# Two pairs of the up projection in two by two steps, with the sums over x1 made in pieces and x1 kept in DRAM

## The chip, the core and the metric

One core of one Trainium2 chip. The metric is the device time of one execution in microseconds, as the median over runs.

## The reference

One layer of a gated convolution and attention block with a convolutional feed-forward part, on 512 positions of width 1024 in float32:

```python
h = rms_norm(x, norm_mix_g[l]);  proj = h @ w_in[l]
... # a gated short convolution and an attention, merged by two gates
x = x + (g_conv * y_conv + g_attn * y_attn) @ w_o[l]
h = rms_norm(x, norm_ffn_g[l])
up = causal_dwconv(h @ w_up[l], conv_ffn_w[l])      # w_up: 1024 x 5632
a, b = jnp.split(up, 2, axis=-1)
x = x + (jax.nn.silu(a) * b) @ w_down[l]            # w_down: 2816 x 1024
...
return rms_norm(x, norm_f_g)
```

## The kernel before

Features lie on the 128 partitions, positions along the free axis; x is 8 blocks of 128 x 512. Float32 products are made of three passes of matmuls: each operand is split into a high and a low part (`wh`, `wl` for weights, `x1h`, `x1l` for the input of the up stage), and high x high, low x high and high x low are added in PSUM. A matmul is 128 x 128 by 256 columns.

**The stream of weights.** All weight chunks stand in one list, `stream`, in the order of use (`in`, `mix`, `wo`, `up`, then `P` and `F` chunks, `dp`). `load` fetches the raw chunk (5 buffers, SP's queue); `split` makes the high part on ACT (`wh_...`) and the low part on DVE (`wl_...`), each with two buffers, so the high part of chunk n+2 is made when PE is through with chunk n. `later` is a list of small pieces of work that `split` lets go behind its own instructions when their turn has come.

**Two by two steps.** Where a stage uses them, two blocks of outputs and two halves of the positions are multiplied by seven products instead of eight (`PROD`, helper `pair`). They need sums of the inputs (four quarter tiles t1 to t4, then their high and low parts) and sums of the weights. The weight sums are made in DRAM, as copies on SP's queue and accumulating transfers on POOL's (`group`, list `todo`), one operation at a time at each `tick`. A step reads a `P` chunk (plain weights) and an `F` chunk (sums). The gates 2 to 7 (`gs`) and most of the down projection (`dn`) are done so; the seven products end in four banks, `p23`, `p45`, `p16`, `p7`, which DVE and ACT put together.

**The wo stage** adds the merged product to x, block by block (`p_wo`): DVE makes x1 (L960), ACT the high part (L961) and the square (L915), DVE the low part (L962), POOL adds the squares to `ssq2` (L916). x1 stays in SBUF.

**The up stage** has 22 pairs of blocks, 0 to 11 in the first phase, each with one block for a and one for b. `block` makes 48 matmuls; with `lead` it does the first two row blocks' eight matmuls with the high weights ahead of the four with `wl`. The first two blocks, up0 and up1, are made by the helper `lead`, which calls `mid` between its parts: there the four matmuls `pc_n2` sum `ssq2` over the partitions, ACT takes the root (a table load and `rb_n2`, L1160) and DVE the reciprocal (L1161). `up` multiplies each block by the norm (`fz`, L992) and applies the three taps (`fu`, L585 on ACT, L586 and L589 on DVE); `glu` takes the silu and POOL or DVE the product; sums of pairs of these (L1022 to L1032) feed the down steps. Each down step adds its banks to x1 (`combine`).

**The end.** The last two blocks of the down projection are made directly, in two halves of the positions (`plain7`). Their sums of squares give the last norm (`fin_sum`, `fin_col`), and `fin_out` multiplies and sends a half away. For the first half the last of four products is POOL's, which reads a copy `rs` of the norm.

**The start.** For the second weight chunk of v (k = 1) DVE casts the first 264 columns (L247) and ACT the other 256 (L249); the matmuls `pa` read the first, `pb` the other. Tile, the layer in which this is written, sets the order of each engine's instructions, except where `keep` holds it; each engine works its list in order.

Of the kernel before, what the change touches and what calls it, by code (L numbers as in the profile page):

```python
# [8 lines left out]
F32 = mybir.dt.float32  # L9
# [4 lines left out]
P = 128  # L14
# [48 lines left out]
def block_kernel(ctx, tc, xT, vecs, wv, win, wmix, wo, wup, wst, wdp, outT):  # L63
# [10 lines left out]
    def keep(ins):  # L74
        return tc.keep_in_program_order(ins)
# [43 lines left out]
    groups = [[NFF + 2 * j, NFF + 2 * j + 1] for j in range(KB - GS)]  # L119
    ngate = len(groups)  # L120
    groups += [list(range(n, min(n + 2, NFF - 1))) for n in range(0, NFF - 1, 2)] + [[NFF - 1]]
    nstep = [len(d) for d in STEPS[0] + STEPS[1]] + [2] * (2 * (KB - GS))
    todo = []
# [26 lines left out]
    for i0, i1 in ((0, ngate), (ngate, len(groups))):  # L150
        for i in range(i0, i1, 3):
            todo += [op for ops in zip(*(group(x) for x in range(i, min(i + 3, i1)))) for op in ops]

    def tick():
        if todo:
            todo.pop(0)()

    def double(n):
        h = nstep[n]
        return [(f"P{n}", wst[n, :, : 3 * h * P], 3 * h * P), (f"F{n}", sums[n][:, : 4 * h * P], 4 * h * P)]  # L160

    def gate_n(j):
# [13 lines left out]
    for ph, (j0, j1) in enumerate(PHASES):  # L176
        stream += [(f"up{j}", wup[j], D) for j in range(2 * j0, 2 * j1)]
        for _ in STEPS[ph]:
            stream += double(n)
            n += 1  # L180
# [48 lines left out]
    def split(hl=None):  # L229

        k = len(parts)
        if k == len(stream):
            return
        nm, _, ncol = stream[k]
        load(k + (LOOK if k >= gs0 else AHEAD))
        if k >= gs0 and (nm[0] in "imwu" or nm[0] == "F" and int(nm[1:]) % 2):
            tick()
        if hl is None:
            hl = []
            for x in "hl":  # L240
                if k == 0:
                    wp.tile([P, PADW[x]], F32, tag=f"pad{x}", name=f"pad_{x}")
                hl.append(wp.tile([P, D], F32R, tag=f"w{x}", name=f"w{x}_{nm}", bufs=2)[:, :ncol])
        hi, lo = hl
        raw = raws[k]
        if k < 2:
            keep(nc.vector.tensor_copy(hi[:, :VW], raw[:, :VW]))  # L247
            if k:
                keep(nc.scalar.activation(hi[:, VW:], raw[:, VW:], AF.Copy))  # L249
# [7 lines left out]
        ins = nc.vector.tensor_sub(lo, raw, hi.bitcast(F32))  # L257
# [5 lines left out]
        run_later(k, {"u": 1.7, "P": 1.6, "F": 0.75, "d": 0}.get(nm[0], 3.5))  # L263

# [111 lines left out]


    ab = ExitStack()
    abp = ab.enter_context(tc.tile_pool(name="abp", bufs=1))
    abp.tile([P, PADL], F32, tag="pad", name="pad_ab")  # L380
    xgh = abp.tile([P, KB, S], F32R, tag="xgh", name="xgh")
    xgl = abp.tile([P, KB, S], F32R, tag="xgl", name="xgl")
    oth = abp.tile([P, 4, S], F32R, tag="oth", name="oth")
# [82 lines left out]
    for kb in range(KB):  # L466
# [16 lines left out]
        for cs in cuts:  # L483
            keep(nc.vector.scalar_tensor_tensor(
                xgl[:, kb, cs], x_of(kb, cs), g1(kb), xgh.bitcast(F32)[:, kb, cs],
                op0=ALU.mult, op1=ALU.subtract,
            ))
# [324 lines left out]
    def mt(name):  # L812
        return mp.tile([P, S], F32, tag="mt", name=name, bufs=5)

# [87 lines left out]
    xp = ctx.enter_context(tc.tile_pool(name="xp", bufs=1, side="right"))  # L902
    x1 = xp.tile([P, KB, S], F32, tag="x1", name="x1")
    x1h = xp.tile([P, KB, S], F32R, tag="x1h", name="x1h")
# [47 lines left out]

    po = None
    for j in range(KB):
        if j == 0:
            po = lead(["wo0", "wo1"], mh, ml)
        p = po[j] if j < 2 else block(f"wo{j}", mh, ml)
        xr = mt(f"xr{j}")
        nc.gpsimd.dma_start(xr, xT[:, j, :])
        nc.vector.tensor_add(x1[:, j, :], p, xr)  # L960
        nc.scalar.activation(x1h[:, j, :], x1[:, j, :], AF.Copy, scale=col(G2 + j))  # L961
        nc.vector.scalar_tensor_tensor(  # L962
            x1l[:, j, :], x1[:, j, :], col(G2 + j), x1h.bitcast(F32)[:, j, :],
            op0=ALU.mult, op1=ALU.subtract,
        )
        square_into(ssq2, x1[:, j, :], j == 0, mp, f"sq2_{j}")
    mg.close()
# [3 lines left out]
    fp = ctx.enter_context(tc.tile_pool(name="fp", bufs=1))  # L971
    fp.tile([P, PADL], F32, tag="pad", name="pad_f")

# [6 lines left out]

    acc = ring(*range(6))
    ssq3 = xp.tile([P, S], F32, tag="ssq", name="ssq3")

    def place(ph, q):
        return (q - PHASES[ph][0] // 2) * (NF + ph)

    def up(j, rb2, pu=None):
        uu = []
        for s_ in range(2):
            p = pu[s_] if pu else block(f"up{2 * j + s_}", x1h, x1l, True)  # L990
            z = fp.tile([P, S], F32, tag="fz", name=f"fz{j}{s_}", bufs=2)
            nc.vector.tensor_mul(z, p, rb2)  # L992
# [57 lines left out]
    def combine(ph, i, banks, ids):  # L1050
# [5 lines left out]
        def z1():  # L1056
            t["z"] = fp.tile([P, S], F32, tag="fz", name=f"cz{ph}{i}", bufs=2)
            nc.scalar.activation(t["z"][:, th[0]], p16[:, th[0]], AF.Copy)
            nc.vector.tensor_add(t["z"][:, th[1]], p16[:, th[1]], t["z"][:, th[0]])
# [4 lines left out]
        def u3():  # L1064
            t["u"] = fp.tile([P, S], F32, tag="fz", name=f"cu{ph}{i}", bufs=2)[:, : 2 * P]
            nc.vector.tensor_add(t["u"], p7, t["z"][:, th[1]])
            nc.vector.tensor_add(m1[:, th[1]], p45[:, th[1]], m1[:, th[1]])
# [17 lines left out]
    def final_square(m):  # L1085
# [8 lines left out]
        nc.scalar.activation(y, y, AF.Copy, scale=col(GF + m))  # L1094

    final_square.first = True
    X, Y = (6, 7, 0, 1), (2, 3, 4, 5)
    open_ = {}

    def down(ph, n0):  # L1100
# [13 lines left out]
        for n, (name, prods) in enumerate(todo):  # L1114
# [98 lines left out]
    def fin_sum(t, m):  # L1213
# [8 lines left out]
        nc.scalar.activation(sq, r, AF.Square)  # L1222
        nc.scalar.activation(y, r, AF.Copy, scale=col(GF + m6 + m))
        return sq
# [7 lines left out]
    def fin_out(t, rc):  # L1232
        hs = halves[t]
        pb = rstd_bc(rc, 2, (1, 4)[t], f"n3{t}")[:, : S // 2]
        if t == 0:
            rs = fp.tile([P, S], F32, tag="fu", name="rs", bufs=3)[:, : S // 2]
            keep(nc.scalar.activation(rs, pb, AF.Copy))
        for g in range(4):
            y = x1[:, 2 * g : 2 * g + 2, hs]
            e, r = (nc.gpsimd, rs) if t == 0 and g == 3 else (nc.vector, pb)  # L1240
            keep(e.tensor_mul(y, y, r.unsqueeze(1).to_broadcast([P, 2, S // 2])))
        for g in range(4):
# [10 lines left out]
    for m in range(2):  # L1253
        plain7(m, 0, kall)
    sqA = [fin_sum(0, 0), fin_sum(0, 1)]
    plain7(0, 1, kall)
    plain7(1, 1, kall[:3])
    rcA = fin_col(0, sqA)
    sqB = [fin_sum(1, 0)]
    plain7(1, 1, kall[3:6])  # L1260
    fin_out(0, rcA)
    plain7(1, 1, kall[6:])
    sqB.append(fin_sum(1, 1))
# [10 lines left out]
def _layout(i):  # L1274
# [51 lines left out]
    for j in range(GS, KB):  # L1326
        for d in range(2):
# [42 lines left out]
```

## Time and profile before

| | |
|---|---|
| median of 3 runs | 697.62 us (697.56 to 697.66) |
| profiled execution | 697.7 us, span 695.9 us |
| PE busy | 686.7 us (99% of the span), 5976 matmuls |
| DVE, ACT, POOL busy | 508.5, 347.7, 158.4 us |
| wo stage | 295 to 338.4 us |
| up, first phase, from | 338.4 us |
| first phase of down | 470.9 to 528 us |
| granted TensorE clock | 0.999 |
| DMA | 118.91 MB, mean 171 GB/s |

Stages are read from the chain in order of time. A row of the timeline has start and duration in us, engine, line of the kernel, operation, output<-inputs by the program's names, shapes, a count (neighbours of one kind are merged) and, in brackets, the idle time before it with what ended it. PEld is the loading of weights, which overlaps PE. A row of a window has its length, the busy time of PE, PEld, DVE, ACT and POOL with counts, the granted clock, the busy share of the DMA engines and GB/s. A row of the groups has the count, the busy time and the mean in ns, then the idle time before.

### The profile page before, as it was taken

To read this page: it belongs to the slowest core of one execution; us is meant where nothing else is said; L and a number is where in the kernel's file an instruction comes from. 1 tells how busy PE (TensorE), PEld (TensorE's weight loads), DVE (VectorE), ACT (ScalarE), POOL (GpSimd) and SP (SyncE) were. 2 spreads that over 40 slices of the span, in tenths; PEclk is the share of its full clock that TensorE was granted. 3 is DMA by queue.
4 is the path that set the end of the run, shared out by engine and by line. 5 is a ranking of instruction groups with operands and counts; after the bars stand their busy time and mean duration, and the time that the engine had idled before them with its cause. 6 is when DMAs were issued, how large, how long until landed. Compare 5 with 4: busy or idle time off the path is not lost.

```text
span 695.9 us, 14568 instructions
## 1 busy us (share of the span) xinstructions
PE 686.7 (99%) x5976; PEld 684.8 (98%) x5976; DVE 508.5 (73%) x807; ACT 347.7 (50%) x553; POOL 158.4 (23%) x179
## 2 busy tenths in 40 slices
PE   8999999999999999999999999999999999999996
PEld 8999999999999999999999999999999999999996
DVE  6678777786687777755387777777684678777785
ACT  6674656554654444444444444445433354445663
POOL 5124646434011001025312212140000212020000
PEclk9999999999999999999999999999999999999999
DMA  8527877567359968768547647488677544433623
GB/s 309 190 86 203 208 154 179 136 172 176 96 147 255 261 178 231 245 187 211 149 110 195 186 120 213 114 177 229 199 210 223 145 99 129 123 96 104 191 78 122
DMA packets 54434, 118.91 MB, mean 171 GB/s; under 512 B 4928, under 2 KB 24384, under 8 KB 54368
## 3 DMA queue, kind: packets, MB, share of 16 engines
q1 hardware_dynamic: 39072, 96.55, 43.1%
q0 software_dynamic: 14576, 20.75, 18.7%
q8 instruction: 47, 0.77, 0.5%
q10 hardware_dynamic: 720, 0.69, 0.3%
q14 instruction: 19, 0.16, 0.1%
HBM read 115.80 MB, written 35.13 MB: 217 GB/s over the span
## 4 chain that ended last, share of the span: by engine, by line
PE 94%; DVE 2%; ACT 2%; issue 1%; DMA 1%; ACTq 0%; SPq 0%; DVEq 0%
PE p_up L286 26%; PE p_in L286 14%; PE dn L304 13%; PE gs L304 8%; PE p_up L304 8%; PE p_wo L286 6%; PE yc L304 3%; PE ya L286 3%; PE p_g L286 2%; PE o L675 2%; PE pa L494 2%; PE pb L496 1%; PE tp L660 1%; PE pdB L286 1%; PE pdA L286 1%
## 5 line engine op out<-in xcount | busy, mean ns | idle before, releaser
L286 PE MATMUL p_up<-x1l,wh_up 128*128 128x256 f32 x536 | 104.5, 276 | 0.0
L286 PE MATMUL p_up<-x1h,wh_up 128*128 128x256 f32 x536 | 104.4, 276 | 0.0
L286 PE MATMUL p_up<-x1h,wl_up 128*128 128x256 f32 x536 | 104.3, 276 | 0.0
L253 ACT ACTIVATE wh_up<-raw_up 128x1024 fp32r<-128x1024 f32 x44 | 46.7, 1060 | 81.8 <-PE p_up L286 68.7
L139 POOL DMA_DIRECT2D sum<-in_wst_dram x51 | 52.7, 1109 | 124.8 <-DMA sum<-sum 88.1
L286 PEld LDWEIGHTS p_up<-x1l,wh_up 128*128 128x128 f32 x536 | 80.8, 188 | 0.0
L286 PEld LDWEIGHTS p_up<-x1h,wh_up 128*128 128x128 f32 x536 | 80.7, 188 | 0.0
L286 PEld LDWEIGHTS p_up<-x1h,wl_up 128*128 128x128 f32 x536 | 80.6, 188 | 0.0
L257 DVE TENSOR_TENSOR wl_up<-raw_up,wh_up 128x1024 fp32r<-128x1024 f32 x44 | 53.8, 1222 | 14.3 <-ACT wh_up L253 14.3
L253 ACT ACTIVATE wh_F<-raw_F 128x1024 fp32r<-128x1024 f32 (+1 forms) x32 | 33.6, 1049 | 58.0 <-PE ya L286 25.8
L286 PE MATMUL p_in<-xgh,wh_in 128*128 128x256 f32 x288 | 56.8, 279 | 0.0
L286 PE MATMUL p_in<-xgh,wl_in 128*128 128x256 f32 x288 | 56.5, 277 | 0.1
L286 PE MATMUL p_in<-xgl,wh_in 128*128 128x256 f32 x288 | 56.5, 277 | 0.0
L992 DVE TENSOR_TENSOR fz<-p_up,rb_n 128x512 f32<-128x512 f32 x44 | 30.3, 690 | 31.5 <-PE p_up L286 31.5
L257 DVE TENSOR_TENSOR wl_F<-raw_F,wh_F 128x1024 fp32r<-128x1024 f32 (+1 forms) x32 | 38.6, 1207 | 20.0 <-ACT wh_F L253 19.8
L286 PEld LDWEIGHTS p_in<-xgh,wh_in 128*128 128x128 f32 x288 | 44.7, 188 | 0.7
L1005 POOL TENSOR_TENSOR ge<-fu,fu 128x512 f32<-128x512 f32 x11 | 17.1, 1553 | 121.4 <-DVE fu L589 107.0
L286 PEld LDWEIGHTS p_in<-xgh,wl_in 128*128 128x128 f32 x288 | 43.5, 188 | 0.3 <-DVE wl_in L257 0.3
L286 PEld LDWEIGHTS p_in<-xgl,wh_in 128*128 128x128 f32 x288 | 43.6, 188 | 0.0
L253 ACT ACTIVATE wh_P<-raw_P 128x768 fp32r<-128x768 f32 (+1 forms) x32 | 26.6, 832 | 27.3 <-PE dn L304 15.0
L304 PE MATMUL p_up<-x1h,wh_up 128*128 128x256 f32 x168 | 40.2, 276 | 0.0
L304 PE MATMUL p_up<-x1l,wh_up 128*128 128x256 f32 x168 | 40.2, 276 | 0.0
(326 smaller groups left out, 2028.5 us busy)
## 6 DMA issues: line engine op xcount, KB each, us to landing
raw_up<-in_wup_dram SPq DMA_DIRECT2D x44, 512.0 KB, 4.4
raw_F<-sum SPq DMA_DIRECT2D x31, 512.0 KB, 4.8
raw_in<-in_win_dram SPq DMA_DIRECT2D x24, 512.0 KB, 4.4
raw_P<-in_wst_dram SPq DMA_DIRECT2D x31, 384.0 KB, 3.4
sum<-in_wst_dram POOLq DMA_DIRECT2D x31, 256.0 KB, 5.6
sum<-in_wst_dram SPq DMA_DIRECT2D x15, 512.0 KB, 5.7
sum<-in_wst_dram POOLq DMA_DIRECT2D x15, 512.0 KB, 8.4
sum<-sum SPq DMA_DIRECT2D x30, 256.0 KB, 6.1
```

The source lines that it names most:

```text
L139: return lambda: keep(nc.gpsimd.dma_start(dst, src, accum_op=ALU.add))
L253: ins = nc.scalar.activation(hi, raw, AF.Copy)
L257: ins = nc.vector.tensor_sub(lo, raw, hi.bitcast(F32))
L286: keep(nc.tensor.matmul(out[:, cs], w, x[:, cs], start=start and i == 0 and c == 0, stop=stop and i == 2 and c == len(cut) - 1,))
L304: keep(nc.tensor.matmul(out, wl if x == 1 else wh, xl if x == 2 else xh, start=opens and bk not in seen, stop=closes and bk not in left,))
L494: keep(nc.tensor.matmul(pa[t][:, :VW], xt, w[:, :VW], start=start, stop=stop))
L496: keep(nc.tensor.matmul(pb[t], xt, w[:, VW:], start=start and t % 2 == 0, stop=stop and t % 2 == 1))
L660: keep(nc.tensor.transpose(tp[:, ks], pt[:, ks], ident))
L675: keep(nc.tensor.matmul(o[:, os_], vv[:, kb, pr, e, :], x[:, kb, cs], start=e == 0 and kb == 0 and i == 0, stop=e == 1 and kb == nk - 1 an ...
L992: nc.vector.tensor_mul(z, p, rb2)
L1005: keep(nc.gpsimd.tensor_mul(ge, a.rearrange(halves_of, h=2), b.rearrange(halves_of, h=2)))
```

## The change

- Pairs 2 and 7 of up (blocks up4, up5, up14, up15) are done with `pair` (chunks P32 to P35, F32 to F35). Their weight sums are made in DRAM with the others; `todo` takes four groups in turn instead of three, and chunks of `mix` and `wo` make two operations each.
- The sums over x1 (`x1_sums`) are made in `later`, for blocks 0 to 5 in the wo stage, from a scaled copy `xs2`; for blocks 6 and 7 at the start of up, from `x3`, read back from DRAM. They are kept in `xf`, the place of the layer's first input.
- x1 is written to DRAM (`x1d`) block by block, and read back after pair 7, into the place of the sums. Up to pair 7 the multiplication by the norm stays in its PSUM bank, later it goes to the free half of that place. Banks go round all eight.
- `mid` is called 12 matmuls earlier.
- The start's two halves for k = 1 change engines. In the end, the first half's norm is asked for one step earlier, its four products are all on DVE, and scalings of the last blocks on ACT come behind their squares.

```diff
+UPS = (2, 7)
...
-        for i in range(i0, i1, 3):
-            todo += [op for ops in zip(*(group(x) for x in range(i, min(i + 3, i1)))) for op in ops]
+        for i in range(i0, i1, 4):
+            todo += [op for ops in zip(*(group(x) for x in range(i, min(i + 4, i1)))) for op in ops]
...
         if k < 2:
-            keep(nc.vector.tensor_copy(hi[:, :VW], raw[:, :VW]))
             if k:
-                keep(nc.scalar.activation(hi[:, VW:], raw[:, VW:], AF.Copy))
+                keep(nc.scalar.activation(hi[:, :VW], raw[:, :VW], AF.Copy))
             else:
-                keep(nc.vector.tensor_copy(hi[:, VW:], raw[:, VW:]))
+                keep(nc.vector.tensor_copy(hi[:, :VW], raw[:, :VW]))
+            keep(nc.vector.tensor_copy(hi[:, VW:], raw[:, VW:]))
...
         part(0, range(KB - 1))
-        part(1, range(4))
+        part(1, range(2))
         if mid is not None:
             mid()
+        part(1, range(2, 4))
         part(0, (KB - 1,))
...
+    def x1_sums(q, x):
+        t1, t3, t4, t2 = b11, b12, b21, b22 = [x[:, a] for a in range(4)]
+        qs = slice(4 * q, 4 * q + 4)
+        def t13():
+            nc.vector.tensor_sub(t1, b11, b12)
+            nc.vector.tensor_sub(t3, b22, b12)
+        def t24():
+            nc.vector.scalar_tensor_tensor(t2, t1, -1.0, b22, op0=ALU.mult, op1=ALU.subtract)
+            nc.vector.scalar_tensor_tensor(t4, t2, -1.0, b21, op0=ALU.mult, op1=ALU.subtract)
+        def hl():
+            nc.scalar.activation(tfh[:, qs], x, AF.Copy)
+            nc.vector.tensor_sub(tfl[:, qs], x, xff[:, qs])
+        k = len(parts) - 1
+        for n, us, f in ((1, 0.85, t13), (1, 0.85, t24), (2, 1.25, hl)):
+            later.append((k + n, us, (("xf", q),), f))
...
-        nc.vector.tensor_add(x1[:, j, :], p, xr)
+        nc.vector.tensor_add(y, p, y)
...
+        nc.gpsimd.dma_start(x1d[:, j, :], y)
+        q, i = divmod(j, 2)
+        if q < 3:
+            if i == 0:
+                xs2 = mp.tile([P, 4, 2 * P], F32, tag="xs2", name=f"xs2{q}", bufs=2)
+            nc.scalar.activation(xs2[:, 2 * i : 2 * i + 2].rearrange("p h c -> p (h c)"), y, AF.Copy, scale=col(G2 + j))
+            if i:
+                x1_sums(q, xs2)
+    flush()
...
+    def up_pair(j):
+        flush([("xf", q) for q in range(4)])
+        p23, p45, p16, p7 = banks = [acc(f"us{j}{i}") for i in range(4)]
+        pair(up_n(j), x1_form, banks)
...
+            nc.scalar.activation(z[:, lo], p16[:, lo], AF.Copy)
+            nc.vector.tensor_add(z[:, hi], p16[:, hi], z[:, lo])
+            nc.vector.tensor_add(u, p7[:, lo], z[:, hi])
+            nc.vector.tensor_add(z[:, hi], p45[:, hi], z[:, hi])
+            nc.vector.tensor_add(p23, p23, z)
+            nc.vector.tensor_add(p45h, p45h, u.unsqueeze(1).to_broadcast([P, 2, S // 2]))
+        if j == UPS[-1]:
+            xg = xfp.tile([P, 4 * KB, 2 * P], F32, tag="xf", name="xg")
+            x1 = xg[:, : 2 * KB].rearrange(whole, h=2)
+            for a in range(0, KB, 4):
+                nc.gpsimd.dma_start(x1[:, a : a + 4, :], x1d[:, a : a + 4, :])
...
+            z = p if j <= UPS[-1] else fz(f"fz{j}{s_}")
...
+    x3 = fp.tile([P, 6, 2 * P], F32, tag="gr", name="x3")[:, :4, :]
+    for i in range(2):
+        y = x3[:, 2 * i : 2 * i + 2].rearrange("p h c -> p (h c)")
+        nc.gpsimd.dma_start(y, x1d[:, KB - 2 + i, :])
+        nc.scalar.activation(y, y, AF.Copy, scale=col(G2 + KB - 2 + i))
+    x1_sums(3, x3)
     for ph, (j0, j1) in enumerate(PHASES):
...
-            e, r = (nc.gpsimd, rs) if t == 0 and g == 3 else (nc.vector, pb)
-            keep(e.tensor_mul(y, y, r.unsqueeze(1).to_broadcast([P, 2, S // 2])))
+            keep(nc.vector.tensor_mul(y, y, pb.unsqueeze(1).to_broadcast([P, 2, S // 2])))
```

The order of instructions is shown at the start of the up stage, on three engines, and behind pair 2, on one. Names end in a buffer's number; `xf` holds the sums over x1, `fu` a block after its taps.

POOL at the end of the wo stage, before:

```order
L916 TENSOR_TENSOR ssq2_4021<-ssq2_4021,sq2_6_4451 128x512
L916 TENSOR_TENSOR ssq2_4021<-ssq2_4021,sq2_7_4515 128x512
L139 DMA sum9_93<-in_wst_dram 256x1x512
L1005 TENSOR_TENSOR ge0_4663<-fu00_4652,fu01_4658 128x512
L139 DMA sum10_94<-in_wst_dram 256x1x512
```

POOL there now:

```order
L934 TENSOR_TENSOR ssq2_4035<-ssq2_4035,sq2_6_4503 128x512
L1007 DMA x1d_4032<-xr7_4429 128x512
L934 TENSOR_TENSOR ssq2_4035<-ssq2_4035,sq2_7_4569 128x512
L1236 DMA x3_4581<-x1d_4032 128x512 x2
L143 DMA sum10_94<-in_wst_dram 256x1x256
L143 DMA sum11_95<-in_wst_dram 256x1x256
```

The write of the last block of x1 stands ahead of POOL's last addition to `ssq2`, and the two loads of x3 behind it.

ACT at the norm of the up stage, before:

```order
L1150 ACTIVATE gh_4524<-ones_70 128x128
L1152 ACTIVATE gh_4524<-ssq2_4021 128x512
L1160 ACT_TABLE_LOAD
L1160 ACTIVATE rb_n2_4617<-pc_n2_4609,ex_101 128x512
L253 ACTIVATE wh_up2_4668<-raw_up2_4390 128x1024
```

ACT there now:

```order
L1251 ACTIVATE gh_4578<-ones_70 128x128
L1253 ACTIVATE gh_4578<-ssq2_4035 128x512
L1237 ACTIVATE x3_4581<-x3_4581,vec_64 128x512 x2
L1261 ACT_TABLE_LOAD
L1261 ACTIVATE rb_n2_4670<-pc_n2_4662,ex_103 128x512
L985 ACTIVATE xf_110<-x3_4581 128x1024
L267 ACTIVATE wh_up2_4731<-raw_up2_4439 128x1024
```

The two scalings of x3 stand ahead of the table load and the root, and the high part of its sums ahead of wh_up2.

DVE at the same place, before:

```order
L1153 TENSOR_TENSOR gl_4525<-ssq2_4021,gh_4524 128x512
L1161 RECIPROCAL rb_n2_4617<-rb_n2_4617 128x512
L257 TENSOR_TENSOR wl_up2_4669<-raw_up2_4390,wh_up2_4668 128x1024
L992 TENSOR_TENSOR fz00_4650<-p_up0_4541,rb_n2_4617 128x512
L992 TENSOR_TENSOR fz01_4656<-p_up1_4542,rb_n2_4617 128x512
```

DVE there now:

```order
L982 SCALAR_TENSOR_TENSOR x3_4581<-x3_4581 128x256
L1262 RECIPROCAL rb_n2_4670<-rb_n2_4670 128x512
L986 TENSOR_TENSOR xf_110<-x3_4581,xf_110 128x1024
L1084 TENSOR_TENSOR p_up0_4606<-p_up0_4606,rb_n2_4670 128x512
L1084 TENSOR_TENSOR p_up1_4607<-p_up1_4607,rb_n2_4670 128x512
L271 TENSOR_TENSOR wl_up2_4732<-raw_up2_4439,wh_up2_4731 128x1024
```

wl_up2 has moved behind the low part of x3's sums and the two multiplications by the norm.

DVE ahead of wl_up8, after pair 2, before:

```order
L257 TENSOR_TENSOR wl_up7_4993<-raw_up7_4727,wh_up7_4992 128x1024
L586 SCALAR_TENSOR_TENSOR fu21_4916<-fz21_4914,vec_64,fu21_4916 128x511
L1032 TENSOR_TENSOR gl_4525<-go0_4790,gh_4524 128x512
L589 SCALAR_TENSOR_TENSOR fu21_4916<-fz21_4914,vec_64,fu21_4916 128x510
L1032 TENSOR_TENSOR gl_4525<-go0_4790,gh_4524 128x512
L992 TENSOR_TENSOR fz30_4983<-p_up6_4934,rb_n2_4617 128x512
L257 TENSOR_TENSOR wl_up8_5062<-raw_up8_4792,wh_up8_5061 128x1024
```

DVE there now, the last twelve of the 19 from wl_up7 on:

```order
L1064 TENSOR_TENSOR us20_4853<-us20_4853,uz2_4977 128x512
L1066 TENSOR_TENSOR us21_4854<-us21_4854,uu2_4978 128x512
L1084 TENSOR_TENSOR us20_4853<-us20_4853,rb_n2_4670 128x512
L1082 SCALAR_TENSOR_TENSOR us21_4854<-us21_4854,rb_n2_4670 128x512
L1084 TENSOR_TENSOR p_up6_4998<-p_up6_4998,rb_n2_4670 128x512
L1124 TENSOR_TENSOR gl_4579<-go0_4851,gh_4578 128x512
L604 SCALAR_TENSOR_TENSOR fu20_4986<-us20_4853,vec_64,fu20_4986 128x511
L604 SCALAR_TENSOR_TENSOR fu21_4991<-us21_4854,vec_64,fu21_4991 128x511
L607 SCALAR_TENSOR_TENSOR fu20_4986<-us20_4853,vec_64,fu20_4986 128x510
L607 SCALAR_TENSOR_TENSOR fu21_4991<-us21_4854,vec_64,fu21_4991 128x510
L604 SCALAR_TENSOR_TENSOR fu30_5048<-p_up6_4998,vec_64,fu30_5048 128x511
L271 TENSOR_TENSOR wl_up8_5128<-raw_up8_4911,wh_up8_5127 128x1024
```

Between wl_up7 and wl_up8 stood 5 instructions, and 17 stand there now: the joining of the pair's banks, its multiplications and all its taps come in.

More of the change, by code (lines that the diff above doesn't have):

```diff
@@ L160, in double, with up_n @@
         return [(f"P{n}", wst[n, :, : 3 * h * P], 3 * h * P), (f"F{n}", sums[n][:, : 4 * h * P], 4 * h * P)]
+    def up_n(j):
+        return [NUP + 2 * UPS.index(j) + d for d in range(2)]
     def gate_n(j):
@@ L176, in block_kernel @@
     for ph, (j0, j1) in enumerate(PHASES):
-        stream += [(f"up{j}", wup[j], D) for j in range(2 * j0, 2 * j1)]
+        for j in range(j0, j1):
+            if j in UPS:
+                for m in up_n(j):
+                    stream += double(m)
+            else:
+                stream += [(f"up{m}", wup[m], D) for m in (2 * j, 2 * j + 1)]
         for _ in STEPS[ph]:
@@ L262, in split @@
         parts.append((hi, lo))
-        run_later(k, {"u": 1.7, "P": 1.6, "F": 0.75, "d": 0}.get(nm[0], 3.5))
+        run_later(k, 0.45 if nm[0] in "PF" and int(nm[1:]) >= NUP else {"u": 1.7, "P": 1.6, "F": 0.75, "d": 0}.get(nm[0], 3.5))
     def chunk(name, hl=None):
@@ L902, in block_kernel @@
     xp = ctx.enter_context(tc.tile_pool(name="xp", bufs=1, side="right"))
-    x1 = xp.tile([P, KB, S], F32, tag="x1", name="x1")
+    x1d = dsp.tile([P, KB, S], F32, tag="x1d", name="x1d")
     x1h = xp.tile([P, KB, S], F32R, tag="x1h", name="x1h")
@@ L1195, in block_kernel @@
     fetch(2)
+    final_square.last = True
     flush()
@@ L1332, in _layout @@
             wst.append(np.concatenate(w, axis=1))
+    for j in UPS:
+        for d in range(2):
+            w = [
+                wup[2 * j + m][:, (2 * q + k) * P : (2 * q + k + 1) * P]
+                for m, k in order for q in (2 * d, 2 * d + 1)
+            ]
+            wst.append(np.concatenate(w, axis=1))
     wst = np.stack(wst)
```

93 lines of the change are left out of this document (65 added, 28 removed).

## The prediction

> **What bounds the kernel now.** I read the page's busy line and its chain first, then the waits of PE, then the chain in order of time.
>
> ```profile
> PE 686.7 (99%) x5976; PEld 684.8 (98%) x5976; DVE 508.5 (73%) x807; ACT 347.7 (50%) x553; POOL 158.4 (23%) x179
> ...
> PE 94%; DVE 2%; ACT 2%; issue 1%; DMA 1%; ACTq 0%; SPq 0%; DVEq 0%
> ```
>
> PE is the bound nearly everywhere, so a matmul left out is worth its whole spacing, and an added wait of PE costs its whole length. The waits of PE, all of them:
>
> ```profile
> PE warm L106 <- DVE ones L98: 1.1, 1, 1.1
> PE pa L494 <- ACT ssq L458: 1.0, 1, 1.0
> PE p_up L304 <- DVE wl_up L257: 0.9, 1, 0.9
> ```
>
> PE waits three times, twice in the start and once where the up stage begins. The change touches the second and the third place. The chain in order of time gives the price of a matmul:
>
> ```profile
> 265.10 9.52 PE gs L304 x84
> ...
> 461.34 4.08 PE p_up L286 x36
> 466.78 4.08 PE p_up L286 x36
> 470.86 57.12 PE dn L304 x504
> ```
>
> A gate pair in two by two steps is 84 matmuls in 9.52 us, 0.1133 each. A direct up block is 461.34 to 466.78, 5.44 us for 48 matmuls, the same 0.1133; two blocks make a pair, 96 matmuls, 10.88 us.
>
> **The pairs (the gain).** Pairs 2 and 7 become 84 matmuls each instead of 96: 24 fewer, 24 x 0.1133 = 2.72 us. The gate pairs already run this form without a PE wait, so the spacing should hold.
>
> **The start of up (the cost).** These rows of the timeline are the third wait of PE and what stands around it; the last rows also show how far apart DVE's instructions start:
>
> ```profile
> 338.57 0.69 DVE L960 TENSOR_TENSOR x<-p_wo,xr 128x512 f32<-128x512 f32 x1 [2.46 <-PE p_wo L286]
> ...
> 340.85 1.87 POOL L916 TENSOR_TENSOR ssq<-ssq,sq 128x512 f32<-128x512 f32 x1 [3.57 <-ACT sq L915]
> ...
> 343.60 1.28 ACT L1160 ACT_TABLE_LOAD   x1
> ...
> 346.53 0.69 ACT L1160 ACTIVATE rb_n<-pc_n,ex 128x512 f32<-128x512 f32 x1 [1.65 <-PE pc_n L1156]
> ...
> 347.26 3.35 DVE L1161 RECIPROCAL rb_n<-rb_n 128x512 f32<-128x512 f32 x1 [2.88 <-ACT rb_n L1160]
> ...
> 350.53 1.16 DVE L257 TENSOR_TENSOR wl_up<-raw_up,wh_up 128x1024 fp32r<-128x1024 f32 x1
> 350.58 0.28 PE L304 MATMUL p_up<-x1l,wh_up 128*128 128x256 f32 x1
> 351.60 1.28 DVE L992 TENSOR_TENSOR fz<-p_up,rb_n 128x512 f32<-128x512 f32 x2
> 351.74 0.74 PE L304 MATMUL p_up<-x1h,wl_up 128*128 128x256 f32 x4 [0.88 <-DVE wl_up L257]
> ...
> 352.80 1.22 DVE L257 TENSOR_TENSOR wl_up<-raw_up,wh_up 128x1024 fp32r<-128x1024 f32 x1
> ...
> 353.93 1.41 DVE L586 SCALAR_TENSOR_TENSOR fu<-fz,vec,fu 128x511 f32<-128x511 f32 x2
> ...
> 355.25 1.40 DVE L589 SCALAR_TENSOR_TENSOR fu<-fz,vec,fu 128x510 f32<-128x510 f32 x2
> ...
> 365.00 0.42 DVE L1022 TENSOR_TENSOR go<-ge 128x256 f32<-128x256 f32 x1
> 365.33 0.75 DVE L589 SCALAR_TENSOR_TENSOR fu<-fz,vec,fu 128x510 f32<-128x510 f32 x1
> ```
>
> Before, PE has done the eight matmuls of up2 that need no wl_up2 by 350.7 (350.58 + 0.11) and goes on at 351.74: it waits 1.04 us, because DVE's reciprocal (3.35 us) stands ahead of wl_up2.
>
> Now ACT has two scalings of x3 ahead of the table load, the root and wh_up2 in its program. They wait for x3, which POOL loads back from DRAM, and POOL may start those loads only when the last x1 block has been written there and its own last addition to ssq2 is through. An engine works its list in order, so the norm and the weights of up2 wait behind this trip through memory. Its parts, from rows of before:
>
> ```profile
> L959 POOL DMA_DIRECT2D xr<-in_xT_dram x8: 548/548/601, 285.8 to 312.4; - x8
> ...
> DMA to landing us min/median/max: 3.0/3.9/6.1
> ```
>
> ```profile
> out_dram<-x SPq DMA_DIRECT2D x6, 256.0 KB, 2.6
> ```
>
> The first fence is the tile xr, loads of 256 KB by POOL's queue, the size and queue of the x3 loads; the second is the list of DMA issues, the nearest row for a write of 256 KB. Block 7 of x1 is ready at 338.57 + 0.69 = 339.26; its write lands at about 339.3 + 2.6 = 341.9. POOL's addition ends at 340.85 + 1.87 = 342.72, later, so that one decides. The two loads are issued at 342.75 and 0.55 later, at 343.3. The second lands at 343.3 + 3.9 = 347.2. For the value I take the median; the ends are 346.3 (3.0) and 349.4 (6.1).
>
> From there (groups by line, for the two instructions that the rows above lack):
>
> ```profile
> L1094 ACT ACTIVATE x<-x,vec 128x512 f32<-128x512 f32 x6 | 4.1, 713 | 0.0
> ```
>
> ```profile
> L818 DVE TENSOR_TENSOR txl<-xq,txh 128x1024 fp32r<-128x1024 f32 x4 | 4.9, 1222 | 1.5 <-ACT txh L817 1.5
> ```
>
> - ACT: scaling 0.71, table load 1.28, root 0.69: 347.2 to 350.0 with 0.05 between them.
> - DVE: the reciprocal 3.35, to 353.4; then, new ahead of wl_up2, the low part of the x3 sums (as L818; 1.13 to the next start, as 352.80 to 353.93) and the two multiplications by the norm (1.20 for both, 351.60 to 352.80), and wl_up2 1.16: to 356.8.
>
> PE goes on at 356.85, 9.65 us after the landing, and had nothing to do from 350.7 but the eight matmuls, wherever wh_up2 lets them stand: a wait of 6.15 us instead of 1.04, **5.1 us lost** (4.2 to 7.3 by the ends of the landing). The norm's four matmuls were moved ahead of 12 others, 12 x 0.1133 = 1.36 us earlier. Alone that could have taken the old wait away; behind the x3 loads it is worth nothing. The four small sums of x3 on DVE lie ahead of the reciprocal, beside the table load, and cost nothing; if x3's second part came alone and late they would still end (4 x 0.42 = 1.7) before the root does (1.28 + 0.69).
>
> **After pair 2 (a second, smaller cost).** PE's need: from the moment R at which it goes on with up2 it has 40 + 48 (up2, up3), 84 (pair), 96 (up6, up7) and 8 matmuls before it needs wl_up8: 276 x 0.1133 = R + 31.3. DVE cannot split up6 before the pair's third weight chunk is free, 148 matmuls or 16.8 us after R; with wh_up6 (1.06) and wl_up6 (1.2) it is at R + 19.0. Up to wl_up8 it then has four small sums (two spaced 0.33, two that wait for the one before, 0.42: 1.5), wl_up7 (1.14), the sums that put the pair's banks together with the parts of the first gated pair between them and the multiplications by the norm (4 small at 0.33, 7 at 0.60, one at 0.66: 6.2), five taps at 0.66 (3.3) and wl_up8 itself (1.2): R + 32.3. PE waits about 1.0 us there. Bounds: nothing, if PE's own pace leaves DVE ahead, and 2.8 us at full durations with no overlap (0.42, 0.69, 0.75, 1.22). I take **1.0**. Pair 7 has fewer sums ahead of wl_up18 (order), and I get no wait there.
>
> **The start.** The second wait of PE:
>
> ```profile
> 6.75 0.72 ACT L471 ACTIVATE xgh<-xs,x 128x512 fp32r<-128x512 f32 x1 [2.08 <-DMA xs<-in_xT_dram]
> ...
> 7.38 0.42 ACT L249 ACTIVATE wh_v<-raw_v 128x256 fp32r<-128x256 f32 x1
> 7.39 0.95 DVE L247 CAST wh_v<-raw_v 128x264 fp32r<-128x264 f32 x1 [1.33 <-DMA raw_v<-in_wv_dram]
> ...
> 8.48 0.72 PE L494 MATMUL pa<-wh_v,xgh 128*128 128x264 f32 x4 [0.97 <-ACT ssq L458]
> ```
>
> PE starts when DVE's cast of the first columns ends, at 8.34; the wait is put down to ACT, which had long cast its half (7.80). The halves change places: PE can begin at about 8.0 with ACT's. The second half is then DVE's, at 8.3, when the first four matmuls (0.45 us) are through. I take **0.4 us gained** (0 to 0.5).
>
> **What costs nothing.** The x1d writes (8 issues on POOL, 0.55 each) and the x1 reload stand beside a POOL busy for 23%. The copies and additions of the weight sums go out in fours instead of threes on SP's and POOL's queues, so each stands further behind the one that it waits for; the raw loads behind them on SP are five buffers ahead of PE. The wo stage gets sums of x1 on DVE and ACT, some 1.5 us more for each of eight blocks on DVE (two small sums at 0.33 or 0.42 and half of an L818), 12 us; the row of the windows for that stage shows DVE busy for half of it:
>
> ```profile
> 295.00:338.00 43.00, 43.00 (x382) 43.00 (x381) 21.78 (x26) 18.30 (x25) 16.97 (x14) 1.00 0.71 200
> ```
>
> The multiplication in place in PSUM is taken at its row, 0.60. In the tail:
>
> ```profile
> 686.37 1.88 DVE L1241 TENSOR_TENSOR x<-x,pb_n 128x512 f32<-128x512 f32 x3 [1.26 <-ACT rs L1237]
> 686.41 1.29 POOL L1241 TENSOR_TENSOR x<-x,rs 128x512 f32<-128x512 f32 x1 [54.42 <-ACT rs L1237]
> ...
> 688.79 0.17 DVE L355 RECIPROCAL rc_n<-ms_n 128x2 f32<-128x2 f32 x1 [0.54 <-ACT ms_n L353]
> ```
>
> A fourth product on DVE (0.62) starts about 0.3 us earlier with the norm and without the copy rs, and fits into the 0.54 us that DVE idles before the second half. PE's matmuls after it are as many as before: 0, within 0.3 either way.
>
> **Sum**, against the profiled execution (697.7, of which the span is 695.9): 697.7 - 2.7 - 0.4 + 5.1 + 1.0 = 700.7. The median of the runs, 697.62, lies 0.08 lower: 700.6.
>
> **Against a rule.** The clock by the windows of the last microseconds:
>
> ```profile
> 689.11 0.61 PE L366 MATMUL pb_n<-ident,rc_n 128*128 128x128 f32 x4
> ```
>
> ```profile
> 693.00:694.00 1.00, 0.00 (x0) 0.00 (x0) 0.00 (x0) 0.00 (x0) 0.00 (x0) 0.94 1.10 387
> 694.00:695.00 1.00, 0.00 (x0) 0.00 (x0) 0.00 (x0) 0.00 (x0) 0.00 (x0) 0.50 0.15 51
> ```
>
> PE's last matmul ends at 689.7, and at about 693.9, 4.2 us later, its clock falls to half. The new wait splits: ACT ends wh_up2 at 351.9 (the high part of x3's sums 1.06 and wh_up2 1.06 after the root), PE does its eight matmuls, and then waits 4.0 us, just under that. The Trainium skill, TensorE: Matmul & The Clock Gate, Part 1, says that the clock is halved after an idle window of about 3.4 us, and that the windows run freely. By that rule a wait of 4.0 us is caught only where a whole window lies in it, and then up to 3.4 us run at half speed, an estimate of 1.7 us more (702.3). The trace agrees with the fall, and shows no recovery.
>
> **Rivals**, with chances.
> 1. The forecast: the trip through DRAM sets the start of up, DVE's backlog a little more. 699.2 to 702.2, likeliest 700.6: 0.52.
> 2. The same wait, but at its least: landing after 3.0 us (4.2 lost) and no backlog. 697.6 - 3.1 + 4.2 = 698.7, no difference that can be told (0.2%, 1.4 us, is about what a measurement of this kernel tells). The least of the xr rows speaks for it, and little else should move just then: 0.20.
> 3. Other side: x3 is back before it hurts. The change gains if PE goes on by 351.74 + 3.1 = 354.85, so if x3 lands by 345.2, 1.9 us after its issue. With a landing at 343.3 (no trip at all) it would be 695.7. Against it: no load of this size on POOL's queue landed in under 3.0. 0.07.
> 4. The clock falls in the wait: if it stays low for as long as it took to fall, 4.2 us at half speed, 2.1 more, 702.7: 0.12.
> 5. The loads land late (6.1), when the additions of the weight sums crowd the queue: 2.2 more, 702.8: 0.09.
>
> Slower by over 0.2%: 1, 4 and 5, 0.73; same 0.20; faster 0.07. The range leaves out 3, a little of 2, and the ends of 4 and 5: 698.3 to 703.0.
>
> **What will show it.** PE's waits: one of about 6 us in total at p_up (by wh_up2 and wl_up2, or by x3), about 1 at wl_up8, and none of 1.0 at pa. ACT: a wait for x3 by DMA just ahead of the root. The pairs: 9.5 us for 84 matmuls. PE: 24 matmuls fewer. I am wrong if ACT's root runs as early as before, or if the loads of x3 land within two microseconds.

## The result, and the profile after

The changed kernel takes 706.13 us (704.92 to 706.63, 4 runs) against 697.64 of the kernel before on the same chip: ratio 1.0118, 95% interval 1.0105 to 1.013. It is slower, as forecast, but by 8.5 us instead of 3.0. The profiled execution is 706.32 with a span of 704.5; of before, 697.7 with 695.9.

The page's busy line and all waits of PE, changed kernel:

```profile
PE 689.0 (98%) x5952; PEld 686.5 (97%) x5952; DVE 534.7 (76%) x842; ACT 359.4 (51%) x570; POOL 168.5 (24%) x196
```

```profile
PE p_up L318 <- DVE wl_up L271: 4.0, 2, 2.9
PE p_up L318 <- ACT wh_up L267: 3.1, 1, 3.1
PE pc_n L1257 <- ACT gh L1253: 1.1, 1, 1.1
PE warm L108 <- DVE ones L100: 1.0, 1, 1.0
PE pc_n L1257 <- DVE gl L1254: 0.3, 1, 0.3
```

24 matmuls fewer, and yet 2.3 us more of PE time: some of the matmuls ran slower. The wait at `pa` is gone. Four of the five waits lie where up begins, one of the two for `wl_up` behind pair 2. The timeline there, by engine (start, duration, and in brackets the idle time before and what ended it):

```profile
339.54 0.56 POOL L1007 DMA_DIRECT2D x1d<-xr  x1
340.41 1.43 POOL L934 TENSOR_TENSOR ssq<-ssq,sq 128x512 f32<-128x512 f32 x1 [0.31 <-ACT sq L933]
344.76 1.12 POOL L1236 DMA_DIRECT2D x<-x1d  x2 [2.93 <-DMA x1d<-xr]
...
344.36 0.31 ACT L1251 ACTIVATE gh<-ones 128x128 fp32r<-128x128 f32 x1 [4.04 <-DMA x1d<-xr]
348.43 0.73 ACT L1237 ACTIVATE x<-x,vec 128x512 f32<-128x512 f32 x1 [3.24 <-DMA x<-x1d]
349.85 0.72 ACT L1237 ACTIVATE x<-x,vec 128x512 f32<-128x512 f32 x1 [0.69 <-DMA x<-x1d]
350.59 1.28 ACT L1261 ACT_TABLE_LOAD   x1
...
345.29 0.47 PE L1257 MATMUL pc_n<-gh 128*128 128x256 f32 x2 [1.08 <-ACT gh L1253]
354.51 0.50 PE L318 MATMUL p_up<-x1h,wh_up 128*128 128x256 f32 x1 [3.14 <-ACT wh_up L267]
359.41 1.22 PE L318 MATMUL p_up<-x1h,wl_up 128*128 128x256 f32 x4 [2.90 <-DVE wl_up L271]
...
394.65 0.74 PE L318 MATMUL p_up<-x1h,wl_up 128*128 128x256 f32 x4 [1.10 <-DVE wl_up L271]
```

The root and `wh_up` of up2 stand behind the scalings of x3 on ACT, and these behind the trip of x1's last block through DRAM. PE goes on with up2's low weights at 359.41 (351.74 before). The chain in order of time (start, length, what), changed kernel:

```profile
294.57 8.17 PE p_wo L300 x72
339.54 4.56 DMA x1d<-xr
345.33 4.49 DMA x<-x1d
352.60 3.35 DVE rb_n L1262
360.63 6.17 PE p_up L300 x36
...
426.73 9.52 PE us L318 x84
...
479.77 57.12 PE dn L318 x504
...
681.39 6.80 PE pdA L300 x60
```

The trip is in the chain now. 36 matmuls at 360.63 take 6.17 us instead of 4.14. Down begins 8.91 later (470.86 before), while the end, from `pdA` to the end of the span, is 0.3 shorter. The same two places in the kernel before:

```profile
352.49 4.14 PE p_up L286 x36
...
672.48 6.80 PE pdA L286 x60
```

The windows (length, PE's busy time with count, granted clock, busy share of the DMA engines, GB/s), first of the changed kernel, then the two same stretches of before:

```profile
340.00:345.00 5.00, 4.21 (x38) 1.00 0.97 296
345.00:350.00 5.00, 4.45 (x36) 1.00 0.90 261
350.00:355.00 5.00, 1.86 (x15) 0.96 0.49 75
355.00:360.00 5.00, 2.10 (x10) 0.50 0.00 0
360.00:365.00 5.00, 5.00 (x25) 0.51 0.46 133
```

```profile
340.00:345.00 5.00, 5.00 (x47) 1.00 0.49 113
345.00:350.00 5.00, 5.00 (x45) 1.00 0.63 98
```

Two things are new: the DMA engines are full in just the stretch in which the trip is made (0.97 and 0.90; 0.49 and 0.63 before), and the clock is at half from 354.65 to 364.85. These two moments by windows of 0.1 us:

```profile
354.60:354.70 0.10, 0.10 (x1) 0.66 0.00 0
...
364.80:364.90 0.10, 0.10 (x3) 0.65 0.61 123
```

The sum from the two traces, up to the start of down: wo starts 0.45 earlier; PE goes on at up2's low weights 7.67 later, 8.12 apart from that gain; the 40 matmuls after it take 1.22 and 6.17 instead of 0.74 and 4.14, 2.5; the wait behind pair 2 is 1.4 with its restart (1.1, and the 40 matmuls behind it take 4.88 instead of 40 x 0.1133 = 4.53); two pairs take 2.72 less. -0.45 + 8.12 + 2.5 + 1.4 - 2.72 = 8.85, of 8.91.

### The profile page after: what moved, and what is told of

Read it like the earlier page. It is cut to its first block, busy times and chain, and to the rows that moved or that the text cites. A ratio compares the mean times of both kernels' runs of the same rounds, so it can differ in the third digit from the quotient of the medians.

```text
span 704.5 us, 14658 instructions
## 1 busy us (share of the span) xinstructions
PE 689.0 (98%) x5952; PEld 686.5 (97%) x5952; DVE 534.7 (76%) x842; ACT 359.4 (51%) x570; POOL 168.5 (24%) x196
## 4 chain that ended last, share of the span: by engine, by line
PE 85%; DVE 6%; ACT 3%; issue 2%; DMA 1%; POOL 0%; ACTq 0%; DVEq 0%; POOLq 0%
PE p_up L300 21%; PE p_in L300 14%; PE dn L318 13%; PE gs L318 8%; PE p_up L318 7%; PE yc L318 3%; PE ya L300 3%; PE us L318 2%; PE pa L512 2%; PE pb L514 2%; PE p_g L300 2%; PE o L693 2%; PE tp L678 1%; PE p_wo L300 1%; PE pdB L300 1%
## 5 line engine op out<-in xcount | busy, mean ns | idle before, releaser
L300 PE MATMUL p_up<-x1h,wh_up 128*128 128x256 f32 x488 | 96.1, 278 | 0.0
L300 PE MATMUL p_up<-x1h,wl_up 128*128 128x256 f32 x488 | 95.9, 278 | 0.0
L300 PE MATMUL p_in<-xf,wh_in 128*128 128x256 f32 x576 | 95.7, 278 | 0.0
L300 PE MATMUL p_up<-x1l,wh_up 128*128 128x256 f32 x488 | 95.7, 278 | 0.0
L300 PEld LDWEIGHTS p_in<-xf,wh_in 128*128 128x128 f32 x576 | 80.4, 188 | 0.7
L300 PE MATMUL p_in<-xf,wl_in 128*128 128x256 f32 x288 | 56.6, 278 | 0.1
L300 PEld LDWEIGHTS p_in<-xf,wl_in 128*128 128x128 f32 x288 | 43.5, 188 | 0.3 <-DVE wl_in L271 0.3
L271 DVE TENSOR_TENSOR wl_P<-raw_P,wh_P 128x768 fp32r<-128x768 f32 (+1 forms) x36 | 34.4, 956 | 10.0 <-PE gs L318 5.4
L318 PE MATMUL p_up<-x1h,wh_up 128*128 128x256 f32 x152 | 37.1, 280 | 3.1 <-ACT wh_up L267 3.1
L318 PE MATMUL p_up<-x1l,wh_up 128*128 128x256 f32 x152 | 37.0, 280 | 0.0
L318 PE MATMUL dn<-gh,wh_F 128*128 128x256 f32 x156 | 36.3, 276 | 0.0
L318 PE MATMUL dn<-gl,wh_F 128*128 128x256 f32 x156 | 36.3, 276 | 0.0
```

Source lines behind the costliest of these rows:

```text
L300: keep(nc.tensor.matmul(out[:, cs], w, x[:, cs], start=start and i == 0 and c == 0, stop=stop and i == 2 and c == len(cut) - 1,))
L318: keep(nc.tensor.matmul(out, wl if x == 1 else wh, xl if x == 2 else xh, start=opens and bk not in seen, stop=closes and bk not in left,))
```

## The experiments

Questions: is it the trip's place in the lists (a), its length (b), or work beside it (c) that costs 8.1; and is the clock's fall a cost of its own (d)?

**x3's scalings behind up2 and up3** (a). The loads stay where they are; ACT's scalings and the sums are held behind the split of up3.

```diff
     x3 = ...
         nc.gpsimd.dma_start(y, x1d[:, KB - 2 + i, :])
-        nc.scalar.activation(y, y, AF.Copy, scale=col(G2 + KB - 2 + i))
-    x1_sums(3, x3)
...
-            glu(ph, j, up(j, nrm["b"], pu))
+            uu = up(j, nrm["b"], pu)
+            if j == 1:
+                for i in range(2):
+                    y = ...
+                    with after_split():
+                        nc.scalar.activation(y, y, AF.Copy, scale=...)
+                x1_sums(3, x3)
+            glu(ph, j, uu)
```

> The changed kernel with one thing moved: ACT's two scalings of x3 and the sums behind them come after the splits of up2 and up3 in the lists; the trip of x3 through DRAM stays. Theory A (the root, and with it the reciprocal and wl_up2, stood behind the trip): PE takes up2 at 351.4 and goes through to the matmuls with wl_up2 at about 352.3 instead of 359.41, and the clock stays at 1.00; 7.1 of waits and about 2.4 of slow matmuls go: 706.1 - 9.5 = 696.6. Theory B (the trip is only part of it; x3's forms are needed by pair 2 at once, and the wait comes back there): PE waits at pair 2's matmuls for xf instead, and the time stays within 3 of 706.

Measured: 699.04 (696.51 to 699.35), ratio to before 1.0011 (1.0 to 1.0021). The place in the lists was worth 7.1 us, all its consequences taken together; theory B, that the wait comes back at pair 2, is out. The waits of PE, and the moments of the clock by windows of 0.1 us:

```profile
PE pc_n L1255 <- ACT gh L1251: 1.7, 1, 1.7
PE p_up L318 <- DVE wl_up L271: 1.2, 1, 1.2
```

```profile
346.90:347.00 0.10, 0.08 (x1) 0.98 1.11 328
347.00:347.10 0.10, 0.10 (x1) 0.50 0.89 358
...
350.40:350.50 0.10, 0.10 (x3) 0.95 0.83 133
```

No wait at up2 is left. But the clock fell here too, which I had not expected: for 3.4 us, after PE had idled for 1.7 and 0.3 us while the norm's `gh` waited for the write of x1's last block, 5.19 in this run. The 2.4 us that this run is above the expected 696.6 are about that half-speed stretch (1.7) and the longer wait (0.6).

**Blocks 6 and 7 from SBUF, no trip** (b against c).

```diff
-        if q < 3:
+        if q < 4:
...
-    x3 = ...
-    for i in range(2): ...
-    x1_sums(3, x3)
```

> The changed kernel with blocks 6 and 7 scaled from the copy in SBUF as blocks 0 to 5 are, so that nothing is read back from DRAM before up; the sums of x3's place stay ahead of the root in the lists of ACT and DVE. Theory A (the trip is the cost): the root runs at about 346.6, no wait of PE at up2, clock 1.00: 696.6. Theory B (DVE's extra work between the reciprocal and wl_up2, and ACT's extra work ahead of the root, are the cost, not the memory): 700 to 703. Under both, the wait of about 1.3 at the norm's matmuls for the write of x1's last block stays.

Measured: 701.72 (701.32 to 702.5), ratio 1.0052 (1.0036 to 1.0069), 4.4 less than the changed kernel. It stands where theory B had it, but for another reason. Rows of the timeline:

```profile
347.82 0.31 ACT L1245 ACTIVATE gh<-ones 128x128 fp32r<-128x128 f32 x1 [1.40 <-DVE xf L986]
348.75 0.77 PE L1251 MATMUL pc_n<-gh 128*128 128x256 f32 x2 [4.27 <-DMA sum<-in_wst_dram]
```

`gh` comes from a pool that is laid over the one of the copy `xs2`, and ACT waits with it until DVE has made the low part of the sums (L986), which reads that copy; PE idles 4.27 us there and its clock is at half from 346.95 to 353.8. (The page names a DMA for PE's wait; ACT's row shows what was late.) With the trip away and the sums still ahead of the norm, the norm waits for the sums instead, so this run doesn't separate b from c.

**Idle time of PE filled** (d).

```diff
                 pu = lead(["up0", "up1"], x1h, x1l, mid)
+                dum = bank(2, "dum")
+                for i in range(56):
+                    keep(nc.tensor.matmul(dum[:, : 2 * P], x1h[:, i % 8, :P],
+                                          x1h[:, i % 8, : 2 * P], start=True, stop=True))
```

> The changed kernel with 56 matmuls of 128x256 on x1h into a free PSUM bank between up1 and up2, 6.3 us of work in the time in which PE waits for x3; their result is used by nobody. Theory A (the half clock from 354.8 to 364.8 came from PE's idle time and cost about 2.4 us in matmuls that were on the path): clock 1.00 all through 340 to 370, 706.1 - 2.4 = 703.7. Theory B (the slow matmuls were covered by the waits for wl_up2): 706.1. Theory C (the clock falls for another reason, as after the DMA burst): clock still 0.50 after 354.8, 706 to 707.

Measured: 704.21 (703.26 to 705.59), ratio 1.0086 (1.0062 to 1.011). Its windows:

```profile
355.00:360.00 5.00, 3.80 (x32) 1.00 0.00 0
360.00:365.00 5.00, 4.83 (x42) 1.00 0.35 107
```

The clock holds, so it was PE's idle time that had lowered it (C is out), and by the medians 1.9 us are gained by doing more work (the runs of the two kernels overlap). In this trace the reciprocal starts at 353.37 instead of 352.60. The trip was not longer (10.2 us from the write's issue to the second landing, 10.3 in the changed kernel); but both scalings stand behind one landing here, 1.34 where 0.72 stood behind the second landing before:

```profile
349.99 1.34 ACT x L1237 x2
```

**The weight sums held back** (b).

```diff
-        if k >= gs0 and (nm[0] in "imwu" or ...):
+        calm = nm in ("wo4", ..., "wo7", "up0", ..., "up3")
+        if k >= gs0 and not calm and (nm[0] in "imwu" or ...):
             tick()
-            if nm[0] in "mw":
+            if nm[0] in "mwu":
                 tick()
```

> The changed kernel with no copies and additions of the weight sums issued at the splits of wo4 to wo7 and up0 to up3; they go out two by two at later up splits. x3 still goes through DRAM in the same place of the lists. Theory A (the write and the read took 4.5 us each because the DMA engines were full): the write of x1's last block lands after about 2.7, the loads after 3.0 to 3.9, PE goes on with wl_up2 at 356 instead of 359.4: 702.8, or 700.4 if the clock holds. Theory B (4.5 us is what this trip takes on POOL's queue): as the changed kernel, 706.1. Theory C (the sums come late for down and stall it): over 707.

Measured: 704.15 (703.9 to 705.6), ratio 1.009 (1.0071 to 1.0109); 2.0 us better than the changed kernel, but short of theory A's 702.8; theory B is out as far as the length goes. Its chain, and the window of that time:

```profile
339.83 3.98 DMA x1d<-xr
344.60 3.24 DMA x<-x1d
```

```profile
340.00:345.00 5.00, 4.95 (x45) 1.00 0.65 199
```

From the write's issue to the second landing it is 8.0 us instead of 10.3. That this is nearly the 7.9 of the prediction is luck in part: the write took 3.98 and still decided, where 2.6 were said, and both loads had landed 3.24 after the first was issued, where 4.45 were said. PE goes on at 358.16, only 1.25 sooner, since both scalings now stand behind one landing; and the clock falls here as well (0.50 from 355 to 360), so that 6.5 us of the loss remain.

**The trip alone, in the kernel before** (b and c).

```diff
         square_into(ssq2, x1[:, j, :], ...)
+        if j >= KB - 2:
+            nc.gpsimd.dma_start(x1d[:, j - KB + 2, :], x1[:, j, :])
...
+    x3 = fp.tile(...)            # as in the change, but without the sums
+    for i in range(2):
+        nc.gpsimd.dma_start(y, x1d[:, i, :])
+        nc.scalar.activation(y, y, AF.Copy, scale=col(G2 + KB - 2 + i))
```

> The kernel before with nothing but a trip added: the last two blocks of x1 are also written to DRAM, read back into a free place, and scaled there by ACT ahead of the root; nothing uses the result, and everything else, the weight sums in threes included, is as before. Theory A (the prediction's arithmetic for the trip holds where the DMA engines have room, 0.39 to 0.63 busy there): write 2.7, loads 3.0 to 3.9, PE goes on with wl_up2 at 353.6 to 354.5 instead of 351.74: 699.5 to 700.4, and up to 1.7 more where the clock falls. Theory B (a trip on POOL's queue takes 4.5 + 4.5 in any case): PE goes on at 356 or later: 702 or more. Theory C (no cost, the trip is beside other work): 697.6.

Measured: 701.7 (699.89 to 702.86), ratio 1.0056 (1.0042 to 1.007). The profiled execution is the 699.89:

```profile
343.01 2.88 DMA x<-x1d
```

```profile
353.89 0.74 PE L304 MATMUL p_up<-x1h,wl_up 128*128 128x256 f32 x4 [2.33 <-DVE wl_up L257]
```

Here the prediction's mechanism comes out: POOL's addition, not the write, releases the loads. They land at 345.9, ahead even of the earliest 346.3 of the prediction, and PE goes on at 353.89, within theory A's 353.6 to 354.5. The clock held in this run although PE idled twice close together, 0.4 us before `wh_up2` and 2.33 before `wl_up2` (the row has all engines, and 1.00 as the clock):

```profile
350.00:355.00 5.00, 2.29 (x17) 2.10 (x18) 5.00 (x5) 1.80 (x3) 0.00 (x0) 1.00 0.15 25
```

The three other runs were 1.65, 1.97 and 2.97 longer with a lower mean clock (0.993 to 0.995 against 0.997). That fits a fall of the clock, but a later landing could have its part in it, and the median of 701.7 lies close to theory B's 702. No trace of them was taken, so this is argued and not shown.

**xr7 out from under gh** (c). The last block of x1 is put in the place of the first norm's tile, which is free by then.

```diff
-            xr.append(mt(f"xr{i}"))
+            xr.append(mt(f"xr{i}") if i < 7 else cp.tile([P, S], F32, tag="rb", name=f"xr{i}"))
```

> The changed kernel with nothing but xr7 moved out from under gh; x3's trip stays ahead of the root. Theory A (what decides the start of up is the trip: write, load, scaling, root, reciprocal, wl_up2, and gh's wait for the write lies beside it): PE has no wait at the norm's matmuls but waits as much more before up2, go-on at 359.4: 706.1 within 0.7 (the clock's windows may fall otherwise). Theory B (gh's wait is a cost of its own): 704.7 or less.

Measured: 706.48 (705.91 to 706.97), ratio 1.0128 (1.0115 to 1.0142): as the changed kernel. As long as the trip decides, the norm's wait for the write lies beside it. It did not go, though: `gh` lies over the place of xr6 too, whose write took 6.93 us.

**x3 behind and xr7 moved**, the two edits together.

> The kernel with x3's scalings and sums behind the splits of up2 and up3, and the last block of x1 (xr7) in the place of the first norm's tile instead of in the pool over which gh is laid. Theory A (gh waited for the write of x1's last block only because it lies over that block, and PE's two waits there, 1.72 and 0.27 us, drew the clock to half for one window of 3.4 us): gh is made at about 342.5, no wait of PE at the norm's matmuls, clock 1.00 from 340 to 370: 699.0 - 2.0 - 1.7 = 695.3. Theory B (gh also lies over xr6, whose write is as late): the wait shrinks to 0.5 or less, 696 to 697. Theory C (the clock falls for another reason): 697.0.

Measured: 696.24 (695.55 to 698.0), ratio 0.9986 (0.9977 to 0.9995), 2.8 less than without the second edit. Theory B: `gh` is still held by xr6's write, PE's idle time there shrinks to 0.5 and 0.3, and the clock stays at 1.00.

**The same with pairs 3 and 7**, `UPS = (3, 7)`.

> As the run with x3 behind and xr7 moved, with the pairs at j = 3 and 7 instead of 2 and 7. Theory A (the wait of 1.1 to 1.2 for wl_up8 comes from what DVE does behind pair 2: the sums of the first gated block, the joining of the pair's banks and the second block's taps all at once): no wait of PE for wl_up behind the pair: 1.1 less, 694.2 if that run gives 695.3. Theory B (any pair leaves DVE as late): the same wait one block later, 695.3.

Measured: 695.08 (694.87 to 695.3), ratio 0.9965 (0.9953 to 0.9978). The wait for `wl_up` behind the pair is gone, and 1.16 us with it. It was the place of pair 2, not the pair.

**The same with pair 7 alone**, `UPS = (7,)`.

> As the run with x3 behind and xr7 moved, with one pair only, at j = 7. Theory A (a pair is worth 12 matmuls, 1.36, where no wait follows it): 1.36 slower than with pairs at 3 and 7 (695.08), 696.4; against pairs at 2 and 7 (696.24), where the wait of 1.1 for wl_up8 took most of the gain, 0.3 slower at most. Theory B (a pair costs or gains something else too): outside 696.0 to 696.9.

Measured: 696.17 (695.52 to 697.18), ratio 0.998 (0.9971 to 0.9989). A pair in a good place is worth 1.09 by the medians (1.36 by count); pair 2 in its place was worth nothing, since 696.24 and 696.17 can't be told apart: its 1.36 go into the wait behind it.

**The start alone, in the kernel before.** Edit: the two lines of the change for k = 1.

> The kernel before with one line of the change: the halves of the second weight block's high part change engines (ACT the first columns, DVE the rest). Theory A (PE's second wait ends earlier by what the chain of the changed kernel showed at wo, 295.02 to 294.57): 697.6 - 0.45 = 697.15. Theory B (the gain is taken back at a later wait): 697.6.

Measured: 697.48 (697.27 to 697.68) against 697.59, ratio 0.9999 (0.999 to 1.0008). The trace shows the gain (wo at 294.68 instead of 295.02, span 695.5 instead of 695.9), the runs don't: 0.1 to 0.4.

**All of it, and the weight sums held back**: x3 behind, xr7 moved, pairs 3 and 7, no sums at wo4 to up3.

> The kernel with x3 behind, xr7 moved and the pairs at 3 and 7 (695.08), and in addition no copies and additions of the weight sums at the splits of wo4 to up3. Theory A (no wait is left at the start of up, so a quicker write of x1 is worth nothing more): 695.1 within 0.4. Theory B (the full DMA engines still hold back gh and the weights): 694.5 or less. Theory C (sums late for pair 3 or down): over 696.

Measured: 693.72 (693.3 to 694.77), ratio 0.9946 (0.9933 to 0.9958); faster than both kernels. All waits of PE that are left, and the start of down:

```profile
PE warm L108 <- DVE ones L100: 1.1, 1, 1.1
PE pa L513 <- ACT wh_v L263: 0.4, 1, 0.4
```

```profile
466.61 57.12 PE dn L319 x504
```

Theory B: the full DMA engines had still cost 1.4. In the run with pairs 3 and 7 but all the sums, the write of the last block was still in the chain, since the root writes the place from which it goes out:

```profile
339.80 5.15 DMA x1d<-xr
```

In the last run PE alone makes the chain there:

```profile
338.23 6.12 PE p_up L301 x54
344.36 0.47 PE pc_n L1256 x4
```

Down begins 4.25 us earlier than in the kernel before: 2.72 for two pairs, 0.31 at the start (wo at 294.71), 1.2 for the old wait at up2 with its restart (4.23 in all). So the change holds the gain that its pairs promise; what surrounded them gave it away.

## Why the prediction was right or wrong

- **Direction and mechanism: right.** ACT's root and `wh_up` of up2 stood behind the trip, and the chain from the landing on was 9.6 us (349.82 to 359.41), where 9.65 was worked out. Undoing the order gave back 7.1 us.
- **The landing, the step that failed first.** The term of the trip was too small. The prediction let POOL's addition decide over the write ("lands at about 339.3 + 2.6 = 341.9"), took 3.9 for the loads and had 347.2. The write took 4.56 and decided; POOL's issue came 0.66 behind its landing, at 344.76 instead of 342.75; the second load took 4.49: 349.82, beyond the range's end of 349.4. So 2.0 of the 2.6 came by the write and 0.6 by the loads. With the start's gain taken apart, the wait cost 8.1 instead of 5.1. The prices came from rows of the kernel before, where the DMA engines had room. The trip alone in that kernel was no dearer than these prices (loads 2.88, and the addition decided), and with the sums held back the changed kernel's trip fell from 10.3 to 8.0.
- **"What costs nothing" was wrong on the weight sums.** In fours, two at a time, they were costed at nothing, with five raw buffers as cover. No wait of PE for raw weights shows, but the sums filled the DMA engines beside the trip: without them the busy share there fell from 0.97 to 0.65. Rival 5 named this crowding, at 0.09.
- **The clock** stood in the sum at nothing (rival 4, 0.12, 2.1 more): it fell, for 10.2 us, and that cost 2.5 us on the path. The prediction treated rivals 4 and 5 as alternatives to the forecast and to each other. Here they came together, which by the prediction's own prices is 700.6 + 2.1 + 2.2 = 704.9, above the range's end of 703.0. A later landing does lengthen the wait, but the clock also fell in the runs with the shorter trip and with x3 behind, so the longer trip was not needed for the fall.
- **The miss in numbers.** 8.5 instead of 3.0: 3.0 by the landing, 2.5 by the clock, 0.4 by the restart behind pair 2, less 0.3 at the end.
- **The norm's four matmuls.** That moving them earlier is worth nothing behind the trip was right; that `gh` lies over the blocks still being written to DRAM was not seen. It costs nothing beside the trip and becomes the bound when that is out of the way.
- **After pair 2:** 1.0 predicted, 1.1 waited and 1.4 lost with the restart. No wait at wl_up18, as said. **Pairs:** 9.52 for 84 matmuls, 2.72, as said. **Start:** 0.45 in the trace, 0.4 said. **Tail:** 0.3 shorter, at the end of the bounds given.

**Against the rule.** The Trainium skill, TensorE: Matmul & The Clock Gate, Part 1, gives an idle window of about 3.4 us as what halves the clock, and free-running windows. The low stretches of the traces last 10.2 (changed kernel), 3.4 (x3 behind) and 6.85 us (no trip), three, one and two times 3.4, so the windows agree. The idle window doesn't: in the run with x3 behind, the clock fell although PE had idled for only 2.0 us of the window before. In the changed kernel it stayed at half over a window with 2.0 us of work (359.41 to 361.45) and rose only after one with work throughout.

## What to carry to other kernels

A trip through DRAM that an engine's list waits for must be priced by how full the DMA engines will be in the changed kernel, not by rows of the kernel before, and it belongs behind everything in the list that PE needs soon. Cases that can feed each other (a late landing, a longer wait, a slower clock) are not alternatives: the range must hold their sum. Look also at what a new tile is laid over: a tile over a buffer that is still being written out waits for that write.

## What the runs showed of the hardware

Two idle spells of 1.7 and 0.3 us within 3.4 us were enough to halve the clock for the next 3.4 (1.7 us lost; x3 behind), while 1.1 and 0.3 (changed kernel) or 0.8 and 0.3 (pair 7 alone) left it at 1.00. The length alone does not decide: 0.4 and 2.33 us left it at 1.00 too, in the run with the trip alone. That the edge of a window cut this idle time in two would explain it; no run shows it. And a write of 256 KB by POOL's queue took 1.7 times as long beside the weight sums. From the DMA issues between 336 and 345 us (count, KB, median us to landing), of the changed kernel and of the last run:

```profile
x1d<-xr POOLq DMA_DIRECT2D x2, 256.0 KB, 5.2
```

```profile
x1d<-xr POOLq DMA_DIRECT2D x2, 256.0 KB, 3.0
```
